# Rotary embedding on one core: the first loads put in one queue behind a 1 MB piece of x, and a small store put ahead of the scalar queue

## The chip, the core and the metric

The kernel runs on one NeuronCore of one Trainium2 chip. The metric is the device time of one execution in microseconds (us): the median of 5 runs. Besides these there is one profiled execution, with a trace of every instruction and of every packet that the core's 16 DMA engines moved. Clock times in this text are microseconds from the start of the profiled span.

## What is computed

The input x has the shape (8, 2048, 8, 64): batch, position, head, element, in float32. The tables cos and sin have the shape (2048, 32). Each head vector of 64 is cut into two halves of 32 and rotated; out has the shape of x.

```python
x1 = x[..., : x.shape[-1] // 2]
x2 = x[..., x.shape[-1] // 2 :]
out1 = x1 * cos - x2 * sin
out2 = x1 * sin + x2 * cos
return np.concatenate([out1, out2], axis=-1)
```

That is 33.55 MB of x read, 33.55 MB of out written, and 0.5 MB of tables read. Every output element needs two products and one sum.

## The kernel before

**Tiles.** The 2048 positions of a batch are spread over 128 partitions, 16 consecutive positions each, so a partition's share of a batch is one contiguous row of 32 KB. A *slab* is half of this for one batch: 8 positions, 4096 floats per partition, 2 MB in all. There are 16 slabs, numbered 0 to 15 in the order of work: first the lower half of all 8 batches, then the upper half (L58). A slab lives in one of 9 buffers `xt` (NBUF, L34), is rotated in place, and is stored from the same buffer. So load 9 has to wait until store 0 has left its buffer, load 10 for store 1, and so on.

**Units.** A slab is rotated in two *units* of 2048 floats per partition (UNIT = 4·HD, HD = 512). Only the first slab (in pieces of HD, HD, 2·HD and UNIT) and the last slab (UNIT, 2·HD, HD, HD) are cut finer (`pieces`, L67). Slab 0 is also loaded in four pieces, 256 KB, 256 KB, 512 KB and 1 MB (`cuts`, L62); every other slab is one load of 2 MB.

**Who does what.** For an ordinary unit (kind A) GpSimd (POOL) makes the two cross products x2·(−sin) and x1·sin into `t2` (L138, two instructions, one with `sin_sb`, one with `nsin`), VectorE (DVE) makes the product of x and cos into `t1` (L144; `cos_ps` is a copy of cos in PSUM, made at L108), and DVE adds the two back into `xt` (L151). In slabs 5 and 10 the sums are made otherwise (L114 to 116): for the first unit (kind C) DVE makes both products (L144, L161), for the second (kind B) DVE makes one and POOL the others; in both, TensorE adds them by products with an identity matrix into PSUM (L156, L157, L172, L173), and ScalarE (ACT) copies the sums back into `xt` (L158, L176). The table `nsin` = −sin is made by ACT (L106).

**Queues.** Loads of x and of sin are issued by SyncE (SP) on its queue, which the profile calls q1 (L84, L89). The load of cos (L92) and all stores (L183) are issued by ACT on its queue, q10. Both queues run on the same 16 DMA engines. A 2 MB transfer is 128 packets of 16 KB, 8 on each engine; a 256 KB transfer is 128 packets of 2 KB.

**Order.** Each engine works through its instructions in order. ACT therefore issues no store while it stands at the copies of slab 5 or of slab 10; the stores behind them, of slabs 3 and 8 and later, are issued right after the last copy. DVE's order is fixed by `keep`, L143 to L164: product, sum, product, sum, unit after unit. The order on POOL is the planner's. The completion of a DMA is counted on one of eight semaphores, which are dealt out in turn, and a DMA waits until the former DMA on its semaphore has landed.

Of the kernel before, what the change touches and what calls it, by code (L numbers as in the profile page):

```python
# [10 lines left out]
def kernel(  # L11
# [7 lines left out]
    nc = tc.nc  # L19
    keep = tc.keep_in_program_order  # L20
    f32 = mybir.dt.float32
    PSUM = bass.MemoryType.PSUM

    B, S, H, D = x.shape
    Dh = D // 2
    P = 128
    HD = H * D
    R = S // P
# [3 lines left out]
    SLAB = SL * HD  # L32
    UNIT = 4 * HD
# [4 lines left out]
    ov = out.rearrange("b (q r) h d -> b q (r h d)", q=P)  # L38
    cos_src = cos.rearrange("(q r) d -> q r d", q=P)
    sin_src = sin.rearrange("(q r) d -> q r d", q=P)  # L40

    const_pool = ctx.enter_context(tc.tile_pool(name="const", bufs=1))
# [7 lines left out]
    cos_sb = const_pool.tile([P, R, Dh], f32, tag="cb")  # L50
# [8 lines left out]
    last = len(slabs) - 1  # L59
    xts = {}  # L60

    def cuts(i):  # L62
        if i == 0:
            return [HD, HD, 2 * HD, UNIT]
        return [SLAB]

    def pieces(i):  # L67
        if i == 0:
            return [HD, HD, 2 * HD, UNIT]
        if i == last:  # L70
            return [UNIT, 2 * HD, HD, HD]
        return [UNIT, UNIT]

    def spans(sizes):
        lo = 0
        for n in sizes:
            yield lo, n
            lo += n

    def load(i):  # L80
        b, l = slabs[i]
        xt = xpool.tile([P, SLAB], f32, tag="xt", name=f"xt{i}")
        for lo, n in spans(cuts(i)):
            nc.sync.dma_start(  # L84
                out=xt[:, lo : lo + n],
                in_=xv[b, :, l * SLAB + lo : l * SLAB + lo + n],
            )
            if i == 0 and lo == 0:
                nc.sync.dma_start(out=sin_sb, in_=sin_src)  # L89
        xts[i] = xt  # L90

    nc.scalar.dma_start(out=cos_sb, in_=cos_src)  # L92
    for i in range(NBUF):
        load(i)

# [2 lines left out]
        out=eye,  # L98
        in_=eye,
# [80 lines left out]
    def store(i, lo, n):  # L180
        b, l = slabs[i]
        keep(
            nc.scalar.dma_start(  # L183
                out=ov[b, :, l * SLAB + lo : l * SLAB + lo + n],
                in_=xts[i][:, lo : lo + n],
            )
        )

    for i in range(last + 1):
        if i == last:  # L190
            for k in range(i - LAG, i):
                store(k, 0, SLAB)
        for lo, n in spans(pieces(i)):
            rotate(i, lo, n)
            if i == last:
                store(i, lo, n)
        if LAG <= i < last:
            store(i - LAG, 0, SLAB)
        if i > LAG and i - LAG - 1 + NBUF <= last:
            load(i - LAG - 1 + NBUF)  # L200
# [30 lines left out]
```

## Time and profile before

| | |
|---|---|
| median of 5 runs | 164.75 us (164.72 to 164.92) |
| the profiled execution's own time | 164.73 us |
| its span in the trace | 162.9 us |
| busy share of the span | DVE 88%, POOL 86%, PE 19%, ACT 7% |
| moved by DMA | 67.66 MB, mean 415 GB/s over the span |
| first instruction of DVE (copy of cos) | 4.89 us |
| first product of POOL | 5.56 us |
| last instruction of DVE ends | 154.79 us |

The profile is read from the outside inwards. The span says how long the traced part lasts; 1.8 us of the run's time lie around it. Then come the busy shares by engine, and the share of the DMA engines in 40 equal slices of the span. A table by stretch gives, for each stretch of time, the busy time of each engine, the granted clock of TensorE, and at its end the mean busy share of the 16 DMA engines and what they moved in GB/s. The DMA view cut to a stretch tells how many packets each queue moved in it. The timeline lists instructions with start and duration; a bracket behind an instruction is the idle time of its engine just before it, and what ended it.

### The profile page before, as it was taken

To read this page: it belongs to the slowest core of one execution; us is meant where nothing else is said; L and a number is where in the kernel's file an instruction comes from. 1 tells how busy PE (TensorE), PEld (TensorE's weight loads), DVE (VectorE), ACT (ScalarE), POOL (GpSimd) and SP (SyncE) were. 2 spreads that over 40 slices of the span, in tenths; PEclk is the share of its full clock that TensorE was granted. 3 is DMA by queue.
4 is the path that set the end of the run, shared out by engine and by line. 5 is a ranking of instruction groups with operands and counts; after the bars stand their busy time and mean duration, and the time that the engine had idled before them with its cause. 6 is when DMAs were issued, how large, how long until landed. Compare 5 with 4: busy or idle time off the path is not lost. (4 is left out here: it accounts for less than half of the span.)

```text
span 162.9 us, 480 instructions
## 1 busy us (share of the span) xinstructions
PE 31.7 (19%) x64; PEld 12.9 (8%) x64; DVE 143.4 (88%) x71; ACT 12.0 (7%) x20; POOL 139.3 (86%) x74
## 2 busy tenths in 40 slices
PE   0000000000000079991000000899900000000000
PEld 0000000000000024440000000344300000000000
DVE  0687999999999999999899999999999999999900
ACT  3300000000000002431000000033210000000000
POOL 1699999999999999799999999956999999995000
PEclk9999999999999999999655555599995555555555
DMA  5999999999999999999999999999999999999995
GB/s 157 372 432 438 414 398 426 418 450 426 418 442 430 426 430 446 422 418 446 422 416 450 424 418 442 442 426 418 446 426 414 446 430 426 430 446 426 414 413 212
DMA packets 5763, 67.66 MB, mean 415 GB/s; under 512 B 640, under 2 KB 640, under 8 KB 1664
## 3 DMA queue, kind: packets, MB, share of 16 engines
q1 hardware_dynamic: 2880, 33.82, 49.6%
q10 hardware_dynamic: 2880, 33.82, 48.7%
q14 instruction: 3, 0.02, 0.0%
HBM read 34.08 MB, written 33.55 MB: 415 GB/s over the span
## 5 line engine op out<-in xcount | busy, mean ns | idle before, releaser
L138 POOL TENSOR_TENSOR t<-xt,sin_sb 128x1024 f32<-128x1024 f32 (+2 forms) x34 | 70.9, 2085 | 10.7 <-DVE xt L151 6.3
L144 DVE TENSOR_TENSOR t<-xt,cos_ps 128x2048 f32<-128x2048 f32 (+2 forms) x36 | 73.9, 2056 | 1.0
L138 POOL TENSOR_TENSOR t<-xt,nsin 128x1024 f32<-128x1024 f32 (+2 forms) x34 | 70.9, 2085 | 0.0
L151 DVE TENSOR_TENSOR xt<-t,t 128x2048 f32<-128x2048 f32 (+2 forms) x32 | 64.8, 2025 | 5.5 <-POOL t L138 2.0
L172 PE MATMUL o<-t,eye 128*128 128x512 f32 x16 | 10.2, 726 | 86.4 <-DVE t L144 86.4
L176 ACT COPY xt<-o 128x512 f32<-128x512 f32 x8 | 4.7, 586 | 93.7 <-PE o L173 93.7
L172 PEld LDWEIGHTS o<-t,eye 128*128 128x128 f32 x16 | 3.6, 238 | 90.7 <-issue 90.7
L156 PE MATMUL o<-t,eye 128*128 128x512 f32 x16 | 8.2, 592 | 0.0
L157 PE MATMUL o<-t,eye 128*128 128x512 f32 x16 | 8.2, 592 | 0.0
L173 PE MATMUL o<-t,neye 128*128 128x512 f32 x8 | 5.7, 799 | 0.2 <-DVE t L161 0.2
L158 ACT COPY xt<-o 128x512 f32<-128x512 f32 x8 | 4.7, 586 | 9.0 <-PE o L157 9.0
L108 DVE COPY cos_ps<-cos_sb 128x512 f32<-128x512 f32 x1 | 0.7, 695 | 4.9 <-DMA cos_sb<-in_cos_dram 4.9
L161 DVE TENSOR_TENSOR t<-xt,sin_ps 128x2048 f32<-128x2048 f32 x2 | 4.6, 2280 | 0.0
L173 PE MATMUL o<-t,eye 128*128 128x512 f32 x8 | 4.1, 592 | 0.0
L156 PEld LDWEIGHTS o<-t,eye 128*128 128x128 f32 x16 | 3.0, 190 | 3.8 <-issue 3.8
L157 PEld LDWEIGHTS o<-t,eye 128*128 128x128 f32 x16 | 3.0, 190 | 3.8 <-issue 3.8
L173 PEld LDWEIGHTS o<-t,neye 128*128 128x128 f32 x8 | 1.8, 252 | 4.3 <-issue 2.7
L173 PEld LDWEIGHTS o<-t,eye 128*128 128x128 f32 x8 | 1.5, 190 | 1.9 <-issue 1.9
L106 ACT ACT_TABLE_LOAD x1 | 1.3, 1283 | 1.2 <-PEq L215 1.2
L106 ACT ACTIVATE nsin<-sin_sb 128x512 f32<-128x512 f32 x1 | 0.6, 630 | 3.0 <-DMA sin_sb<-in_sin_dram 3.0
L109 ACT COPY sin_ps<-sin_sb 128x512 f32<-128x512 f32 x1 | 0.6, 579 | 0.0
L96 POOL MEMSET eye<- 128x128 f32 x1 | 0.2, 205 | 0.3 <-POOLq L215 0.3
(6 smaller groups left out, 1.0 us busy)
## 6 DMA issues: line engine op xcount, KB each, us to landing
xt<-in_x_dram SPq DMA_DIRECT2D x15, 2048.0 KB, 29.5
out_dram<-xt ACTq DMA_DIRECT2D x15, 2048.0 KB, 16.1
xt<-in_x_dram SPq DMA_DIRECT2D x1, 1024.0 KB, 7.6
out_dram<-xt ACTq DMA_DIRECT2D x1, 1024.0 KB, 10.5
xt<-in_x_dram SPq DMA_DIRECT2D x2, 256.0 KB, 4.2
xt<-in_x_dram SPq DMA_DIRECT2D x1, 512.0 KB, 5.6
out_dram<-xt ACTq DMA_DIRECT2D x1, 512.0 KB, 9.1
out_dram<-xt ACTq DMA_DIRECT2D x2, 256.0 KB, 7.7
```

What stands on the lines that cost most here:

```text
L106: nc.scalar.mul(nsin, sin_sb, -1.0)
L108: nc.vector.tensor_copy(cos_ps, cos_sb)
L138: nc.gpsimd.tensor_mul(out=t2u[:, :, u, :].rearrange("p (r h) d -> p r h d", h=H), in0=xu[:, :, 1 - u, :].rearrange("p (r h) d -> p r h d" ...
L144: nc.vector.tensor_mul(out=t1.rearrange("p (r k d) -> p r k d", r=nr, d=Dh), in0=xk, in1=rep(cos_ps[:, r0 : r0 + nr, :], 2 * H),)
L151: keep(nc.vector.tensor_add(out=xt, in0=t1, in1=t2))
L156: nc.tensor.matmul(o, eye, t1[:, cs], start=True, stop=False)
L157: nc.tensor.matmul(o, eye, t2[:, cs], start=False, stop=True)
L158: keep(nc.scalar.copy(xt[:, cs], o))
L161: nc.vector.tensor_mul(out=t2.rearrange("p (r k d) -> p r k d", r=nr, d=Dh), in0=xk, in1=rep(sin_ps[:, r0 : r0 + nr, :], 2 * H),)
L172: nc.tensor.matmul(o, eye, t1u[:, gs, u, :], start=True, stop=False)
L173: nc.tensor.matmul(o, eye if u else neye, t2u[:, gs, 1 - u, :], start=False, stop=True)
L176: keep(nc.scalar.copy(xu[:, gs, u, :], o.rearrange("p (g d) -> p g d", d=Dh)))
```

## The change

The load of cos moves from ACT's queue to SP's queue. On SP's queue the order becomes: the first 1 MB of slab 0, cos, sin, the second 1 MB of slab 0, then the slabs as before. Slab 0 is rotated in pieces of 2·HD, 2·HD and UNIT, the last slab in UNIT, 2·HD and 2·HD, and the last slab is stored in two transfers of 1 MB instead of 1 MB, 512 KB, 256 KB and 256 KB. A tile of zeros is set by DVE, and ACT's queue begins with a store of 16 x 16 zeros (64 bytes from each of 16 partitions) to a place in out that the store of the last slab writes later.

```diff
+    zero = const_pool.tile([P, 16], f32, tag="zero")
+    nc.vector.memset(zero, 0.0)
+    nc.scalar.dma_start(out=ov[B - 1, 0:16, R * HD - 16 : R * HD], in_=zero[0:16, :])
+
     def cuts(i):
-        if i == 0:
-            return [HD, HD, 2 * HD, UNIT]
-        return [SLAB]
+        return [UNIT, UNIT] if i == 0 else [SLAB]
 
     def pieces(i):
         if i == 0:
-            return [HD, HD, 2 * HD, UNIT]
+            return [2 * HD, 2 * HD, UNIT]
         if i == last:
-            return [UNIT, 2 * HD, HD, HD]
+            return [UNIT, 2 * HD, 2 * HD]
         return [UNIT, UNIT]
...
             if i == 0 and lo == 0:
+                nc.sync.dma_start(out=cos_sb, in_=cos_src)
                 nc.sync.dma_start(out=sin_sb, in_=sin_src)
         xts[i] = xt
 
-    nc.scalar.dma_start(out=cos_sb, in_=cos_src)
     for i in range(NBUF):
         load(i)
...
         for lo, n in spans(pieces(i)):
             rotate(i, lo, n)
-            if i == last:
-                store(i, lo, n)
+            if i == last and lo == 0:
+                store(i, 0, UNIT)
+        if i == last:
+            store(i, UNIT, UNIT)
```

In the built program of the changed kernel POOL's first products come in another order. Before, they were, piece by piece of slab 0, sin then nsin: s0, n0, s1, n1, s2, n2, s3, n3. Now they are s0, s1, n0, n1, s2, n2, with pieces of twice the size. The order on DVE is as written: product and sum of piece 0, product and sum of piece 1, and so on. From slab 1 on, the orders on all engines are those of before.

## The prediction

> **What bounds the kernel now.** I began with the page's slices of the span, because two engines stand near 90% and the DMA queues move 67.66 MB.
>
> ```profile
> DMA  5999999999999999999999999999999999999995
> GB/s 157 372 432 438 414 398 426 418 450 426 418 442 430 426 430 446 422 418 446 422 416 450 424 418 442 442 426 418 446 426 414 446 430 426 430 446 426 414 413 212
> ```
>
> The DMA engines are never idle between the second slice and the last. The chain that ended last names DVE for 17% and DMA for 13%, but it ends with DVE at 154.79, and 8 us of span follow in which only stores run. So the transfers set the end, and the second view is the table by stretch: where do they move less than their usual rate?
>
> ```profile
> 1.50:3.00 1.50, 0.00 (x0) 0.00 (x0) 0.00 (x0) 0.94 (x1) 0.00 (x0) 1.00 0.63 149
> 3.00:4.50 1.50, 0.00 (x0) 0.00 (x0) 0.00 (x0) 0.00 (x0) 0.00 (x0) 1.00 1.05 395
> 4.50:6.00 1.50, 0.00 (x0) 0.00 (x0) 1.07 (x2) 0.56 (x2) 0.44 (x1) 1.00 1.04 306
> 6.00:9.00 3.00, 0.00 (x0) 0.00 (x0) 2.17 (x4) 0.79 (x3) 3.00 (x5) 1.00 1.04 406
> 18.00:22.00 4.00, 0.00 (x0) 0.00 (x0) 3.90 (x2) 0.00 (x0) 4.00 (x2) 1.00 1.02 381
> 80.00:117.00 37.00, 14.48 (x30) 6.20 (x31) 36.19 (x17) 3.86 (x7) 33.64 (x16) 0.65 1.01 431
> 124.00:156.00 32.00, 0.00 (x0) 0.00 (x0) 29.62 (x17) 0.00 (x0) 24.72 (x15) 0.50 1.00 429
> ```
>
> The last two columns are the DMA share and GB/s. Full rate is 431. Against it the stretches lose (431 - rate)/431 of their length: 0.98, 0.13, 0.44 and 0.17 us up to 9 us, and 0.46 us at 18 to 22, when the first store joins the loads. Elsewhere almost nothing is lost, so about 2 us is all that the transfers could gain.
>
> The third view is the timeline, for the other bound. DVE and POOL run without a pause from slab 1 on, so a late start of theirs is still there at slabs 5 and 10, where ACT stands at its copies and the stores wait behind them.
>
> ```profile
> 5.56 0.73 POOL L138 TENSOR_TENSOR t<-xt,sin_sb 128x256 f32<-128x256 f32 x1 [4.25 <-DMA sin_sb<-in_sin_dram]
> 17.67 2.30 DVE L144 TENSOR_TENSOR t<-xt,cos_ps 128x2048 f32<-128x2048 f32 x1
> 73.88 0.59 ACT L158 COPY xt<-o 128x512 f32<-128x512 f32 x1 [1.13 <-PE o L157]
> 73.89 1.85 ACTq L183 DMA_DIRECT2D out_dram<-xt  x4
> 118.44 1.86 ACTq L183 DMA_DIRECT2D out_dram<-xt  x4
> ```
>
> At 73.89 and 118.44 ACT issues the stores of slabs 3 and 8. How long could they be late before the DMA engines run dry? The DMA view, cut to 118.4 to 121.3 and to 121.3 to 122.7, answers for the second:
>
> ```profile
> q1 hardware_dynamic: 80, 1.31, 105.4%
> q10 hardware_dynamic: 2, 0.00, 0.0%
> ...
> q10 hardware_dynamic: 25, 0.41, 68.2%
> q1 hardware_dynamic: 19, 0.15, 25.0%
> ```
>
> Columns: packets, MB, share. The new store moves nothing until 121.3; the last load has 0.15 MB left then, 0.35 us at full rate. All loads are done after that. So without the store the engines would have been dry at about 121.7.
>
> **The change part by part.**
>
> *Transfers, start.* Before, four transfers of 2 KB packets lead; now 8 KB packets do, with only the tables' 512 KB in 2 KB packets. The first 0.98 us of loss (first packets on their way) I keep. Of the other 0.74 us I let 0.5 go, since a queue of bigger packets is not short of work; bounds 0 (if the gap at 4.5 to 6 comes from something else) and 0.74.
>
> *Transfers, first store.* The first store is issued at 17.66; from 17.7 to 21.5 the DMA view shows q1 packets alone, 384 GB/s. No such loss shows at 73.89 (423 GB/s from 72 to 77), so it belongs to the first store to out or on that path. The store of zeros has 16 rows and may pay it at the start. There it either overlaps the 0.98 us that is lost anyway (gain 0.46) or delays the loads by as much (gain 0). I take half, 0.23.
>
> *Transfers, end.* The last 1 MB leaves in 8 KB packets rather than 4 KB and 2 KB. 395 against 431 GB/s on 0.5 MB of 2 KB packets is 0.11 us; I take 0.1. Sum of the transfers' lead: 0.5 + 0.23 + 0.1 = 0.8 us.
>
> *Issues.* SP issues cos as well, 0.40 us on ACT in the row of before, ahead of sin, the second half of slab 0 and all later loads; the first 1 MB takes 2.4 us to move, so the queue behind it is never empty and this costs nothing. ACT's zero store waits for a small memset on DVE; behind it stand only the table load and nsin, which waits for sin anyway. Load 4 waits for the zero store's semaphore; its turn comes after 20 us, so that wait is covered unless that store takes over 15 us.
>
> *Compute, start.* POOL starts when sin has landed. Before, three transfers of 256 KB had to pass; now 1.5 MB, which is 0.79 MB more, 1.82 us at 431 GB/s. POOL's start P becomes 5.56 + 1.82 = 7.4; bounds 6.9 (if the 2 KB ramp's loss goes) and 7.9 (if the zero store costs its 0.46 here). POOL's products of 128x512 followed each other by 1.22 us before (8.28, 9.50, 10.71), those of 128x1024 by 2.29. DVE's first sum needs n0, the third of the new order: it ends at P + 2.44 + 1.25 = P + 3.7. From there DVE works without a wait: sum (1.24), product and sum of piece 1 (1.27 each, n1 is ready), product of the unit (2.3) and, with the pauses of some 0.03 to 0.1 between, the sum from P + 9.95 (n2 has ended at P + 9.47) to P + 12.25. So the first product of slab 1 starts at P + 12.27 = 19.65, against 17.67: DVE is 2.0 us late (bounds 1.5 and 2.5), and stays so, since slab 1 and later are unchanged and DVE has no pauses there to make it up.
>
> *What that costs.* Nothing, while transfers are queued. The stores of slab 8 are issued at 118.44 + 2.0 = 120.44. At an empty queue a transfer takes about 0.9 us to its first packets (SP's first issue at 0.74, first bytes in the stretch 1.5 to 1.75; cos, issued at the same time, about 1.3). They are ready at 121.3 to 121.7. The loads run dry at 121.7 less the lead. So the stores can be 2.4 us late at most without loss; with 2.0 us, the lead that survives this place is 0.4 us of the 0.7 that exists there. At slab 3 the same sum (0.31 MB left at 77.1, so dry at 77.8; issue 73.89) leaves 3.0 us; it does not decide. At the end, DVE's last three pieces take 0.45 us less (two instructions fewer), it ends at 156.3, and the last 1 MB store is ready at 157.2; its turn comes at about 158.6. Covered.
>
> *Sum.* 164.73 - 0.4 - 0.1 = 164.2 us; the profiled execution is within 0.02 us of the median of runs, so that is also the forecast for it.
>
> A rule beside this: the stores of 17.66, 73.89 and 118.44 waited 3.9, 3.3 and 2.9 us for their first packets while loads were queued. [...]
>
> **Rivals.**
>
> *Full gain.* The zero store takes the whole 0.46 us, the start all of 0.74, and DVE is only 1.5 us late, because the loads start sooner. Then the transfers lead by 1.2 us, and of that 2.4 - 1.5 = 0.9 survives slab 8: 164.73 - 0.9 - 0.1 = 163.7. For it: the big packets lead. Against it: it needs all at once.
>
> *Only moved.* The losses at 4.5 to 6 and 18 to 22 stay or reappear elsewhere, the lead is 0.1 to 0.2: 164.6.
>
> *Late stores: slower.* If the 2.9 to 3.9 us from issue to first packet is a fixed delay of a store and not the queue in front of it, the stores of slab 8 come 2.0 us later whatever the loads do. At 118.44 there is then only 0.35 us of cover; the rest, 1.65 us, is dry DMA time, less 0.1 at the end and plus the lead, which is lost too: 164.73 + 1.65 - 0.1 = 166.3. It decides from 0.35 us of lateness on. For it: both late places show about 3 us. Against it: a load issued at 84.41, into an empty q1 while q10 was busy, moves next to nothing in the stretch up to 87.8 either (9 packets, 0.02 MB), while the first load of all needed 0.9; so it is the other queue's packets that delay, not a store's nature. A milder form, DVE 2.5 us late and 1.3 us to the first packet, leaves 2.0 us of cover for 2.5 of lateness: 164.73 + 0.5 - 0.1 = 165.1.
>
> **How the numbers follow.** Forecast (164.0 to 164.5) 0.42, full gain 0.15, only moved or no change (164.5 to 165.05) 0.25, late stores 0.18. What a measurement of this kernel can tell from no change is about 0.2%, 0.33 us: faster is below 164.42. The forecast's upper edge reaches past it, so faster 0.42 - 0.06 + 0.15 = 0.51; same 0.25 + 0.06 - 0.02 = 0.29; slower 0.18 + 0.02 = 0.20. The range runs from 163.5, the full gain less 0.2 for the coarse reading of the dry time at a window's edge, to 165.6, where the milder late stores are in and half of the full late case is out.
>
> **What would show it.** Right: POOL's first product near 7.4, slab 1's first product on DVE near 19.65, the stores of slabs 3 and 8 issued near 75.9 and 120.4; 4.5 to 6 and 18 to 22 above 400 GB/s; no stretch under 90% DMA share around 77 and 121. Wrong: a dry stretch there (late stores), a loss of 0.4 us that stays at the first store (the zero store does not pay it), or a DVE that makes up its lateness before slab 5.

## The result and the profile after

The changed kernel takes 165.53 us (median of 24 runs, 164.69 to 169.5) against 164.75 us before (43 runs beside them). The ratio is 1.0045 with a 95% interval of 1.0033 to 1.0057: slower by 0.45%, where I had forecast 164.2 us. The profile that was taken first of the changed kernel is of a disturbed execution (169.5 us, one DMA engine ends 3 us behind the next), so all lines here are of the run *again*, the same kernel: profiled 165.36 us, span 163.5 us. Line numbers of the changed kernel are two above those of before (L144 is L146).

In the page's slices, the DMA engines are again busy from the second slice to the last:

```profile
DMA  5999999999999999999999999999999999999996
GB/s 192 411 451 417 441 309 417 437 433 433 421 441 433 425 433 433 437 417 437 433 429 427 437 415 429 437 429 425 425 385 409 449 405 429 449 405 429 449 385 257
```

Slice two is better than before (411 against 372), slice six is much worse (309 against 398, at 20.4 to 24.5 us), and so is slice 30 (385, at 118.5 to 122.6 us). The table by stretch, with the stretches of before and three more (last two columns: DMA share, GB/s):

```profile
1.50:3.00 1.50, 0.00 (x0) 0.00 (x0) 0.00 (x0) 1.11 (x1) 0.00 (x0) 1.00 0.85 224
3.00:4.50 1.50, 0.00 (x0) 0.00 (x0) 0.00 (x0) 0.00 (x0) 0.00 (x0) 1.00 1.02 427
4.50:6.00 1.50, 0.00 (x0) 0.00 (x0) 0.00 (x0) 0.00 (x0) 0.00 (x0) 1.00 0.95 352
6.00:9.00 3.00, 0.00 (x0) 0.00 (x0) 1.92 (x2) 1.31 (x3) 1.86 (x2) 1.00 1.08 455
18.00:22.00 4.00, 0.00 (x0) 0.00 (x0) 3.86 (x3) 0.00 (x0) 4.00 (x3) 1.00 1.02 401
22.00:26.00 4.00, 0.00 (x0) 0.00 (x0) 3.97 (x2) 0.00 (x0) 4.00 (x3) 1.00 0.99 328
121.00:122.00 1.00, 0.58 (x2) 0.00 (x0) 1.00 (x1) 0.38 (x1) 1.00 (x1) 1.00 0.77 328
122.00:123.00 1.00, 0.00 (x0) 0.00 (x0) 0.97 (x2) 0.20 (x1) 1.00 (x2) 1.00 0.63 262
124.00:156.00 32.00, 0.00 (x0) 0.00 (x0) 30.86 (x16) 0.00 (x0) 26.20 (x14) 0.50 1.00 426
```

Before, the stretches 22 to 26, 121 to 122 and 122 to 123 moved 414, 377 and 508 GB/s. So the start gained, the first store to out lost more than that stretch ever had, and at 121 to 123 the engines were partly dry. The timeline has the lateness of the compute:

```profile
7.14 2.47 POOL L140 TENSOR_TENSOR t<-xt,sin_sb 128x512 f32<-128x512 f32 x2 [5.84 <-DMA sin_sb<-in_sin_dram]
10.85 1.22 DVE L153 TENSOR_TENSOR xt<-t,t 128x1024 f32<-128x1024 f32 x1 [2.66 <-POOL t L140]
19.43 2.29 DVE L146 TENSOR_TENSOR t<-xt,cos_ps 128x2048 f32<-128x2048 f32 x1
75.39 3.60 ACTq L185 DMA_DIRECT2D out_dram<-xt  x4
121.68 2.23 ACTq L185 DMA_DIRECT2D out_dram<-xt  x3
```

POOL starts 1.6 us later than before, DVE's first sum stands 2.66 us for the third product of POOL, and DVE reaches slab 1 1.76 us later. The stores of slab 3 are issued 1.5 us later and those of slab 8 3.24 us later. The DMA view of 121 to 123 us, 40 slices of 0.05 us in which a packet is counted where it starts, shows the result:

```profile
DMA  9997970077797777700000000000009997000000
```

From 121.85 to 122.5 us no engine starts a packet: the loads are done and the stores of 121.68 have not come yet. A packet of 16 KB usually took 0.61 us, and by the packets the engines stood idle for up to 1.25 us here, some 0.55 us in the mean.

### The profile page after: what moved, and what is told of

The parts are those of the page before. It is cut to its first block, busy times and chain, and to the rows that moved or that the text cites. A ratio compares the mean times of both kernels' runs of the same rounds, so it can differ in the third digit from the quotient of the medians.

```text
span 167.6 us, 462 instructions
## 1 busy us (share of the span) xinstructions
PE 33.7 (20%) x64; PEld 13.5 (8%) x64; DVE 142.8 (85%) x68; ACT 12.0 (7%) x20; POOL 138.6 (83%) x70
## 5 line engine op out<-in xcount | busy, mean ns | idle before, releaser
L140 POOL TENSOR_TENSOR t<-xt,sin_sb 128x1024 f32<-128x1024 f32 (+1 forms) x32 | 70.1, 2191 | 10.7 <-DMA sin_sb<-in_sin_dram 5.6
L146 DVE TENSOR_TENSOR t<-xt,cos_ps 128x2048 f32<-128x2048 f32 (+1 forms) x34 | 73.5, 2168 | 1.0
L140 POOL TENSOR_TENSOR t<-xt,nsin 128x1024 f32<-128x1024 f32 (+1 forms) x32 | 70.1, 2193 | 0.0
L153 DVE TENSOR_TENSOR xt<-t,t 128x2048 f32<-128x2048 f32 (+1 forms) x30 | 64.5, 2149 | 6.1 <-POOL t L140 2.6
L174 PE MATMUL o<-t,eye 128*128 128x512 f32 x16 | 11.7, 824 | 87.0 <-DVE t L146 87.0
L158 PE MATMUL o<-t,eye 128*128 128x512 f32 x16 | 8.2, 592 | 0.0
L159 PE MATMUL o<-t,eye 128*128 128x512 f32 x16 | 8.2, 592 | 0.0
L175 PE MATMUL o<-t,neye 128*128 128x512 f32 x8 | 6.2, 866 | 0.1
L175 PE MATMUL o<-t,eye 128*128 128x512 f32 x8 | 4.1, 592 | 0.0
L158 PEld LDWEIGHTS o<-t,eye 128*128 128x128 f32 x16 | 3.0, 190 | 3.8 <-issue 3.8
```

The costliest lines, as they stand in the source:

```text
L140: nc.gpsimd.tensor_mul(out=t2u[:, :, u, :].rearrange("p (r h) d -> p r h d", h=H), in0=xu[:, :, 1 - u, :].rearrange("p (r h) d -> p r h d" ...
L146: nc.vector.tensor_mul(out=t1.rearrange("p (r k d) -> p r k d", r=nr, d=Dh), in0=xk, in1=rep(cos_ps[:, r0 : r0 + nr, :], 2 * H),)
L153: keep(nc.vector.tensor_add(out=xt, in0=t1, in1=t2))
L158: nc.tensor.matmul(o, eye, t1[:, cs], start=True, stop=False)
L159: nc.tensor.matmul(o, eye, t2[:, cs], start=False, stop=True)
L174: nc.tensor.matmul(o, eye, t1u[:, gs, u, :], start=True, stop=False)
```

## The experiments

Each row below is one kernel: the start of DVE's first product of slab 1; when the stores of slabs 3 and 8 were issued; the loss of the DMA engines in three places of its profile; the profiled time; median and ratio to the kernel before on the same chip. A loss here is the length of a stretch less the usual time of the packets in it (16 KB 0.611, 8 KB 0.309, 4 KB 0.159, 2 KB 0.084 us), the mean of 16 engines: *start* from the first packet (1.72 to 1.76 us) to 9 us, *first store* 18 to 27 us, *late* 72 to 124 us, the last as the difference to before. For after_held, whose first packet comes at 2.98 us, the start is counted from where that of the others begins. All in us. A profile is one execution: those of after_nozero and after_11 lie below the median of their runs, that of after_order is its slowest run.

| kernel | DVE slab 1 | stores 3 / 8 | start | first store | late | profiled | median, ratio |
|---|---|---|---|---|---|---|---|
| before | 17.67 | 73.89 / 118.44 | 1.33 | 0.48 | 0 | 164.73 | 164.75 |
| again | 19.43 | 75.39 / 121.68 | 0.63 | 1.20 | 0.71 | 165.36 | 165.36, 1.0026 (1.001 to 1.0042) |
| after_nozero | 19.25 | 75.64 / 120.02 | 0.70 | 1.19 | 0.16 | 164.93 | 165.25, 1.0026 (1.0003 to 1.0049) |
| after_cosact | 19.24 | 76.00 / 120.58 | 0.62 | 0.98 | 0.53 | 165.24 | 165.35, 1.0025 (1.0002 to 1.0048) |
| after_order | 18.99 | 76.51 / 121.09 | 0.60 | 1.32 | 0.67 | 166.35 | 165.28, 1.0031 (1.0013 to 1.0048) |
| after_11 | 19.35 | 75.44 / 120.03 | 0.67 | 1.04 | 0.16 | 164.64 | 165.35, 1.0036 (1.0011 to 1.0062) |
| after_held | 20.68 | 77.45 / 121.83 | 1.80 | 1.11 | 0.59 | 166.44 | 166.33, 1.0104 (1.0074 to 1.0133) |
| after_early | 16.86 | 73.80 / 118.17 | 0.66 | 0.74 | 0 | 164.24 | 164.38, 0.9980 (0.997 to 0.9991) |
| before_zero | 17.72 | 74.00 / 118.34 | 1.18 | 0.57 | 0 | 164.80 | 165.29, 1.0013 (0.9999 to 1.0026) |
| before_tail | 17.60 | 74.09 / 118.64 | 1.35 | 0.28 | 0 | 164.63 | 164.88, 1.0003 (0.9994 to 1.0012) |
| before_cossp | 18.52 | 75.26 / 119.81 | 1.11 | 0.80 | 0 | 165.43 | 165.35, 1.0025 (1.0007 to 1.0044) |
| before_late | 18.52 | 76.20 / 120.75 | 1.23 | 0.62 | 0.49 | 165.51 | 164.98, 1.0005 (0.9992 to 1.0019) |
| before_late3 | 20.46 | 76.98 / 121.53 | 1.44 | 0.53 | 0.96 | 165.54 | 166.15, 1.0071 (1.0054 to 1.0088) |
| before_1mb | 19.02 | 75.60 / 119.97 | 0.63 | 1.07 | 0.31 | 165.05 | 165.40, 1.003 (1.001 to 1.0051) |
| before_512 | 17.98 | 74.30 / 118.64 | 0.70 | 0.85 | 0 | 164.31 | 164.62, 0.9983 (0.9974 to 0.9993) |
| again_512 | 18.27 | 74.86 / 119.20 | 0.71 | 0.74 | 0 | 164.27 | 164.47, 0.9991 (0.9975 to 1.0008) |
| before_512_11 | 18.22 | 74.68 / 119.02 | 0.83 | 0.77 | 0 | 164.39 | 164.62, 0.9994 (0.9983 to 1.0005) |
| before_10 | 18.70 | 74.85 / 119.20 | 0.92 | 0.73 | 0 | 164.59 | 164.59, 0.9998 (0.9982 to 1.0014) |
| before_12 | 18.05 | 74.89 / 119.44 | 1.30 | 0.53 | 0 | 164.70 | 164.82, 1.0006 (0.9995 to 1.0016) |

My theory after the result was that the stores of slabs 3 and 8 come too late for the DMA queues. The rival was that one of the transfers at the start (the zero store, cos on the sync queue, the large first piece) makes the loss by itself.

**again**, the changed kernel unchanged.

> The changed kernel once more, unchanged, for a profile whose time is near the median of 165.5. Late stores: POOL's first product near 6.9, slab 1's first product on DVE near 19.2, the stores of slabs 3 and 8 issued near 76.3 and 120.9, and a DMA share under 0.9 for some 0.5 to 1 us near 77 to 79 or 121 to 124. Zero store to blame: no such dip, but a loss at the start or at the first store that before doesn't have. Time 165.5 in both.

Measured 165.36 us. Slower once more, and the spread of the changed kernel is wider (164.8 us upwards) than that of before.

**after_nozero**, the change without the store of zeros:

```diff
-    zero = const_pool.tile([P, 16], f32, tag="zero")
-    nc.vector.memset(zero, 0.0)
-    nc.scalar.dma_start(out=ov[B - 1, 0:16, R * HD - 16 : R * HD], in_=zero[0:16, :])
```

> The changed kernel without its store of zeros. Late stores: 165.3 to 165.6, as the changed kernel, since DVE is as late as there. Zero store to blame: 164.3 to 164.8, the loss goes. If the store of zeros had helped at the first store: 165.7 to 166.

165.25 us, a first store of 1.19 us. Without the zero store the first real store loses as much as with it.

**before_zero**, the kernel before with the same three lines behind the load of cos.

> The kernel before, with the store of zeros added behind cos on the scalar queue. Late stores: 164.75 as before, or 164.3 if the zeros pay for the loss at the first store (381 GB/s at 18 to 22). Zero store to blame: 165.2 to 165.6.

First store 0.57 against 0.48 us, median 165.29 us with a ratio whose interval takes in 1. Neither way does the zero store pay for the first store, which is what my term of 0.23 us stood on. The median by itself lies where I expected it if the zero store were to blame (165.2 to 165.6 us); what speaks against that is after_nozero, which is as slow without the store. Why this median lies above the profiled 164.80 us I can't say.

**before_late**, the kernel before with one product of POOL ahead of the others, into a tile that nobody reads, and **before_late3** with three, of which this is the edit:

```diff
+    late = const_pool.tile([P, R, Dh], f32, tag="late")
+    for _ in range(3):
+        keep(nc.gpsimd.tensor_mul(out=late, in0=sin_sb, in1=sin_sb))
```

> The kernel before, with one more product of 128x512 on POOL ahead of its first one (1.25 us, into a tile that nobody reads); its result is not used. The loads are those of before, only the compute is later, by some 1.3 us. Late stores: 165.2 to 166. If lateness is hidden behind queued transfers, as I forecast (2.4 us of cover): 164.75.

> The kernel before with three more products of 128x512 on POOL, whose result is not used, ahead of and among its first ones; DVE some 3.3 us late. Late stores with 2.4 us of cover at 118.44: stores of slab 8 issued near 122, a dry stretch of 1 to 1.5 us there, time 165.7 to 166.3. If lateness never costs: 164.75 to 165.

With DVE 0.85 us late the median is 164.98 us, no difference that can be told (its profile, 165.51 us, is of one of the slower runs); with DVE 2.79 us late it is 166.15 us, 0.71% slower. Here every transfer is that of before, so lateness by itself makes the kernel slower. Its first store, issued 2.8 us later, still loses only 0.53 us: the first store's loss is not made by lateness. Where the lateness shows, in the table by stretch and the timeline of before_late3:

```profile
86.00:90.00 4.00, 0.00 (x0) 0.00 (x0) 3.86 (x3) 0.00 (x0) 4.00 (x2) 0.50 1.03 389
76.98 7.39 ACTq L186 DMA_DIRECT2D out_dram<-xt  x5
```

and the same stretch before:

```profile
86.00:90.00 4.00, 0.00 (x0) 0.00 (x0) 3.90 (x2) 0.00 (x0) 4.00 (x3) 0.50 1.00 428
```

428 against 389 GB/s: most of the loss isn't where the late stores are issued but 10 us further on, where load 12 starts up beside them. There some 16 packets of the store queue took up to 0.6 us longer than the usual 0.611, which is 0.5 us in the mean of the engines. Another 0.26 us is lost at 77.8 to 80 us, where the late stores of slab 3 have their first packets: seven of these are longer too, by up to 0.9 us.

**after_cosact**, the change with cos on the scalar queue, behind the zero store (not ahead of it, as the expectation says), and **before_cossp**, the kernel before with cos on the sync queue behind the first 256 KB:

```diff
+    nc.scalar.dma_start(out=cos_sb, in_=cos_src)
...
             if i == 0 and lo == 0:
-                nc.sync.dma_start(out=cos_sb, in_=cos_src)
                 nc.sync.dma_start(out=sin_sb, in_=sin_src)
```

> The changed kernel with the load of cos back on the scalar queue, ahead of the zeros; x and sin as changed. Cold queue (the first transfer of 128 packets on the scalar queue costs its loss at whatever time it comes, and 16 small packets don't pay it): the loss at 18 to 26 us falls from 1.2 to about 0.6 us, time 164.6 to 164.9. Late stores alone: DVE is as late as in the changed kernel, so 165.3 to 165.5.

> The kernel before with the load of cos moved to the sync queue behind the first 256 KB of x, nothing else. Cold queue: the loss at 18 to 26 us grows from 0.6 to about 1.2 us and the time to 165.3. Late stores alone: sin lands 0.1 us later at most, 164.75 to 165.

165.35 us both. Where cos is loaded doesn't decide it: the changed kernel stays slow with cos back on its queue. That before_cossp is slow as well isn't explained by its losses (none late). The losses are means of the 16 engines, but the time ends with the last engine, and the engines end unevenly. In before_cossp the last packet ends at 162.46 us and the engines in the mean at 161.2; in before these are 161.78 and 161.0, in after_order 163.10 and 161.7, in again 162.07 and 162.0. So the last engine is 0.1 to 1.4 us behind the mean, and most of the 0.6 and 0.8 us by which the profiled times of before_cossp and after_order lie above what their losses give is this. Why the engines end so far apart I leave open.

**after_order**, the change with POOL's order kept as written (sin, nsin, sin, nsin):

```diff
-                nc.gpsimd.tensor_mul(
+                keep(nc.gpsimd.tensor_mul(
```

> The changed kernel with POOL's first products in the order sin, nsin, sin, nsin of pieces 0 and 1. DVE's first sum no longer waits for the second sin product: DVE about 0.5 us late rather than 1.6. Late stores: the dry stretch near 122 is gone in every run, time 164.9 to 165.2. Cold queue alone: 165.2 to 165.4, the first store's loss stays at 1.2 us.

DVE reaches slab 1 0.44 us sooner than in again, the time stays: 165.28 us. No dry stretch shows near 122 us in its profile, and still the time isn't the 164.9 to 165.2 us that I expected with that.

**after_held**, the change with the first load held back by a memset of DVE on the same buffer (128x1024, work that the change doesn't have) and the loads kept in the order as written:

```diff
+        if i == 0:
+            nc.vector.memset(xt[:, 0:HOLD], 0.0)
```

> The changed kernel with its first load held back by a memset of 128x1024 on DVE into the same buffer, so that all loads start about 1 us later. In the ten profiles so far the loss of the transfers up to 9 us and that at 18 to 27 us (the first store) add up to 1.9 to 2.4 us, whichever is large. Time limit (the loads are held to a fixed amount by about 27 us, so what is gained at the start is lost at the first store): the loss at 18 to 27 us falls from 1.2 to 0.3 or 0.5 us and the time stays at 165.4 to 165.7. Two separate losses: 1.2 us stays, time 166.2 to 166.6.

The first load is issued 1.25 us later than in again, and all that follows with it. The start loses 1.80 us instead of 0.63, the first store still 1.11 us, and the time is 166.33 us, 1.0 us more. So the first store's loss isn't a limit on how far loads may get by a certain time, or a later start would have made it smaller. Counted from its own first packet, the start of after_held loses 0.65 us, as again's does.

**before_1mb** is the kernel before with slab 0 loaded in two pieces and POOL's order kept, **before_512** with three, **before_tail** with the end of the change alone (last slab in UNIT, 2·HD, 2·HD and two stores). The first lines of the two loads:

```diff
-            return [HD, HD, 2 * HD, UNIT]
+            return [UNIT, UNIT]            # before_1mb
+            return [2 * HD, 2 * HD, UNIT]  # before_512
```

> The kernel before with slab 0 loaded in two transfers of 1 MB, cos on the scalar queue and all pieces as before, POOL's order of before kept. Loss goes over: start 0.8 us instead of 1.7, first store 1.1 instead of 0.5, and DVE about 1.2 us late; time 164.9 to 165.3. If the first store's loss belongs to cos on the sync queue or to the coarser pieces: it stays at 0.5 and the time is 164.2 to 164.5.

> The kernel before with slab 0 loaded as 512 KB, 512 KB, 1 MB, sin behind the first; a step half way. DVE about 0.5 us late, so stores of slabs 3 and 8 below the lateness from which loss was seen. Loss goes over: 164.6 to 165. If a start gain can be kept when the stores are in time: 164.2 to 164.5, faster than both kernels.

> The kernel before with the end of the changed one alone: last slab rotated as UNIT, 2 HD, 2 HD and stored in two transfers of 1 MB. By my sum 0.1 us faster, 164.6 to 164.8. If one 1 MB store at the end lets the slowest DMA engine finish later: 164.9 to 165.2.

The large first piece alone makes the kernel as slow as the whole change does: 165.40 us, start 0.63, first store 1.07, DVE 1.35 us late. The 512 KB piece keeps nearly all of the start's gain with DVE 0.31 us late: 164.62 us, ratio 0.9983. The table by stretch of before_512 has both sides of it, the start (332 before) and the first store (408 before):

```profile
1.50:9.00 7.50, 0.00 (x0) 0.00 (x0) 2.94 (x5) 2.29 (x4) 3.12 (x5) 1.00 1.01 382
18.00:27.00 9.00, 0.00 (x0) 0.00 (x0) 8.76 (x4) 0.00 (x0) 9.00 (x5) 1.00 0.99 380
```

The end of the change is worth nothing that can be told: 164.88 us beside 164.88, where the interval of the ratio (0.9994 to 1.0012) would hide 0.1 us.

Two things were open then: why the first store's loss goes with how slab 0 is loaded (0.3 to 0.6 us where 256 KB lead, 0.85 where 512 KB, 1.0 to 1.3 where 1 MB), and whether lateness is the whole of the slowdown. Four kernels vary the number of DMAs on the sync queue and the leading piece apart:

```diff
+ after_11:       [UNIT, 2 * HD, 2 * HD]
+ before_12:      [HD, HD, 2 * HD, 2 * HD, 2 * HD]
+ before_512_11:  [2 * HD, HD, HD, UNIT]
+ before_10:      [HD, 3 * HD, UNIT]
```

> The changed kernel with the second 1 MB of slab 0 loaded as 512 KB and 512 KB, so that the sync queue takes one DMA more before the first store. If the number of DMAs in the sync queue decides the first store's loss (18 to 27 us), the loss falls from 1.2 us to about 0.5 to 0.9 us and the time to about 164.8 to 165.1 us. If the size of the leading piece decides, the loss stays at 1.0 to 1.2 us and the time at 165.3 to 165.5 us.

> The kernel before with the last 1 MB of slab 0 loaded as 512 KB and 512 KB: one DMA more in the sync queue, the leading piece of 256 KB kept. If the number decides, the first store's loss moves away from 0.5 us (cos on the sync queue also made one DMA more, and gave 0.8 us): about 0.8 us and 165.1 us. If the size of the leading piece decides, the loss stays at 0.3 to 0.6 us and the time at 164.8 us.

> The kernel before with slab 0 loaded as 512 KB, 256 KB, 256 KB and 1 MB: a leading piece of 512 KB with the number of DMAs of before. If the number decides, the first store's loss is 0.5 us and not the 0.85 us of the three-piece load led by 512 KB; the start keeps most of its gain, and the time is 164.1 to 164.4 us, the best so far. If the leading piece decides, the loss is 0.85 us and the time 164.6 us.

> The kernel before with slab 0 loaded as 256 KB, 768 KB and 1 MB: the leading piece of 256 KB kept, one DMA fewer. If the number decides, the first store's loss rises to 0.85 to 1.2 us and the time to 165.1 to 165.5 us. If the leading piece decides, the loss stays at 0.3 to 0.6 us and the time at 164.7 to 164.9 us.

First stores of 1.04, 0.53, 0.77 and 0.73 us. The number of DMAs falls: one more left the changed kernel at 1.04 and the kernel before at 0.53. The size of the leading piece fits three of the four, but before_10, led by 256 KB, lies between (0.73). What the loss does follow, roughly, is the gain of the start: 0.3 to 0.6 us where the start loses 1.2 to 1.4 (before_cossp: 0.8 at 1.1), 0.7 to 0.85 where it loses 0.7 to 0.9, 1.0 to 1.3 where it loses 0.6 to 0.7. Both together are 1.81 us before and 1.83 in again, and 1.4 to 2.0 in all other kernels but after_held (2.91), whose first packet was made later by force.

**after_early**, the change without lateness. The two products of POOL for the first piece of slab 0 are left out, and DVE's sum of that piece adds x itself; all transfers are those of the change. In the first piece out is then not the rotated x:

```diff
+        lone = i == 0 and lo == 0
-        if kind != "C":
+        if kind != "C" and not lone:
...
-            keep(nc.vector.tensor_add(out=xt, in0=t1, in1=t2))
+            keep(nc.vector.tensor_add(out=xt, in0=t1, in1=xt if lone else t2))
```

> The changed kernel with less work at its start: the two products of POOL for the first piece of slab 0 are left out, and DVE's sum of that piece adds x itself in their place, so that POOL is done with slab 0 about 2.5 us sooner; all transfers are those of the changed kernel. DVE's first product of slab 1 should start near 17.0 us (19.4 us in the changed kernel, 17.67 before). If lateness makes the changed kernel slower, the losses behind 72 us go, the first store's loss of 1.1 to 1.3 us stays and only cancels the gain at the start, and the time is 164.5 to 164.9 us, the time before. If something else makes it slower, the time stays at 165.2 to 165.5 us. If my first forecast had only missed the lateness, the lead of the start would survive and the time would be 164.2 us or less.

164.38 us, ratio 0.998, and the runs lie between 164.21 and 164.8 us. Its timeline and its table by stretch:

```profile
16.86 2.29 DVE L147 TENSOR_TENSOR t<-xt,cos_ps 128x2048 f32<-128x2048 f32 x1
73.80 1.89 ACTq L186 DMA_DIRECT2D out_dram<-xt  x4
118.17 1.92 ACTq L186 DMA_DIRECT2D out_dram<-xt  x4
```

```profile
18.00:27.00 9.00, 0.00 (x0) 0.00 (x0) 8.72 (x5) 0.00 (x0) 9.00 (x5) 1.00 0.99 388
117.00:126.00 9.00, 1.07 (x3) 0.19 (x1) 8.74 (x5) 0.58 (x1) 9.00 (x5) 0.68 1.01 433
```

and the last stretch in again:

```profile
117.00:126.00 9.00, 4.58 (x11) 1.71 (x9) 8.74 (x5) 1.81 (x4) 8.93 (x5) 0.90 0.94 397
```

117 to 126 us moves 433 GB/s (397 in again), and all late loss is gone. The same transfers are 1.0 us faster by the medians, 0.8 us by the two ratios to before, once DVE reaches slab 1 2.57 us sooner, which is 0.81 us ahead of before. That it has to be ahead isn't the point: before_512, before_512_11, before_10 and before_12 have DVE 0.3 to 1.0 us late and lose nothing behind 72 us either. The first store still loses 0.74 us, so that is a loss of its own, but smaller than the 1.2 us of again. My expectation of 164.5 to 164.9 us was too high by that.

**again_512**, before_512 once more.

> The three-piece load of slab 0 led by 512 KB in the kernel before, once more: it gave 164.62 us and a ratio of 0.9983, while its two relatives with a leading piece of 512 KB in four pieces and of 256 KB in three gave 0.9994 and 0.9998. If the gain is real, the ratio is again 0.998 to 0.999 with an interval below 1; if it was chance, the interval takes in 1.

164.47 us, ratio 0.9991 with an interval from 0.9975 to 1.0008. Two profiles of 164.27 and 164.31 us against 164.73 speak for a small gain, but only one of two intervals lies below 1. A version that beats both kernels by 0.1 to 0.2% is likely, not shown.

## Why the prediction was wrong, step by step

- **Transfers set the end**: right. after_early and before_512 gain (ratios 0.998 and 0.9983) where the transfers gain.
- **Start, 0.5 us (0 to 0.74)**: right in its place, 0.70 us measured. Part of it came from 1.5 to 3 us (149 to 224 GB/s), which I had kept as lost; 4.5 to 6 us reached 352 GB/s, not 400.
- **First store, "I take half, 0.23"**: wrong in sign. The loss grew from 0.48 to 1.20 us. The store of zeros changes nothing there (after_nozero 1.19), so no run shows the mechanism that I priced; the bounds of 0 to 0.46 left out a loss, with no reason for it. The loss goes roughly with the start's gain and is as large in again.
- **End, 0.1 us**: not shown; before_tail gives no difference, but could not tell 0.1 us.
- **POOL's start 7.4, DVE's first product of slab 1 at 19.65**: 7.14 and 19.43, inside the bounds. DVE is 1.76 us late where I said 2.0; the chain of durations held.
- **"The stores of slab 8 are issued at 118.44 + 2.0 = 120.44"**: failed. They were issued at 120.02 to 121.68 us in the profiles of again and of the variants of the change whose DVE is 1.6 to 1.8 us late. The lateness of DVE isn't passed on one to one, because the copies of ACT wait for TensorE (9.0 us in all ahead of those of L158 on the page of before), whose clock comes up at different times. The table by stretch of again and of before, 106 to 111 us (third column from the right: granted clock):

```profile
106.00:111.00 5.00, 4.94 (x7) 2.04 (x7) 4.91 (x4) 0.58 (x1) 3.80 (x2) 0.54 1.00 423
```

```profile
106.00:111.00 5.00, 5.00 (x13) 2.21 (x12) 4.91 (x3) 1.76 (x3) 2.07 (x1) 1.00 0.98 419
```

  Clock 0.54 against 1.00: 7 matmuls against 13, one copy against three. Cut to half-microsecond stretches, the table has the full clock 3.2 us (after_11), 3.4 (before), 4.0 (before_late3), 5.3 (after_early) and 6.4 us (again) behind the first matmul of slab 10, with 3.2 us between the ends. The lengths themselves come in steps: in all 20 traces the full clock lasts 13.65 or 17.07 us at a time and the half clock between the two bursts 27.31 or 30.72 us, which is 4, 5, 8 and 9 times 3.41 us. What sets the wait for the full clock isn't shown.

  Which wait a run met shows in its mean granted clock, without a trace. In the five profiled runs with a mean under 0.79 the full clock at slab 10 came 5.3 to 6.4 us behind the first matmul, in the other fifteen 3.2 to 5.0 us. The changed kernel, four variants of it and before_1mb, all with DVE 1.3 to 1.8 us late, have 91 runs under 168 us: the 38 with a mean under 0.79 have a median of 165.51 us, the other 53 one of 165.06. This speaks for the wait for the full clock as a part of the slowdown, not the whole; in the runs of before the same difference goes either way, by up to 0.3 us.
- **Slab 8, cover 2.4 us**: about right. Stores issued at 121.09 (after_order) and 121.53 us (before_late3) lost 0.06 and 0.12 us between 117 and 124, at 121.68 (again) 0.59. Cover ends some 3 us behind 118.44.
- **Slab 3, "leaves 3.0 us; it does not decide"**: wrong. No kernel whose stores of slab 3 were issued up to 75.26 us lost anything behind 72 us; from 75.4 on all of them lose there: 0.1 to 0.3 us up to 75.64 (again without its dry stretch at slab 8), 0.5 to 0.7 at 76.0 to 76.5, 0.96 at 76.98 (after_held left aside, whose loads are late as well). The cover is some 1.4 us, and what ends it isn't a dry stretch at 77.8, the only thing that I had priced, but longer packets of the stores, where load 12 starts and behind it (in before_late3 from 77.8 us on as well).
- **The lead that survives, 0.4 us**: 0 in the changed kernel, since the first store takes back 0.72 of the 0.70 us. In after_early 0.67 us at the start less 0.26 at the first store, 0.41 us, survive, and its 164.24 us profiled lie 0.49 under before.
- **Rivals**: *late stores* had the right sign, and its milder form (165.1) came near, but by luck. Its 0.5 us of dry time is there in again, but it came from stores 3.24 us late behind a DVE 1.76 us late, with 0.8 us to their first packets, where the rival had 2.5, 2.5 and 1.3 us. A store's delay isn't fixed at 3 us: that of 121.68 had packets at 122.5 us, as I had taken it. *Only moved* describes the start and the first store.
- **The stores' waits of 3.9, 3.3 and 2.9 us**: by the packets of before, 4.06, 3.42 and 3.02 us from the issue to the first of them. In again the first store waited 4.45 us.

So two steps failed. The first-store term was priced as a gain of 0.23 us and was a loss of 0.72 us in again; that is 0.95 us off, and it took the start's lead away. The cost of lateness was priced at 0.4 us of that lead and nothing more. DVE's 1.76 us were right, but 0.71 us were lost between 72 and 124 us: 0.12 us between the start of load 12 and 117 us, where I had ruled out a loss, and 0.59 us at slab 8, whose stores came 1.24 us later than my sum had them. Both hang on when the compute starts: in after_early, with the same transfers, the first loss is 0.46 us smaller and the second is gone, and with them the whole slowdown (165.36 to 164.38 us). The account isn't closed to the last tenth: in again another 0.3 us is lost behind 124 us, the engines end 0.98 us later in the mean than before, and the time is 0.63 us longer, since in before the last engine is 0.8 us behind the mean and in again 0.1.

Not settled: why loads that started sooner lose more at the first store. In every kernel the loss lies in packets of loads that take longer, at most by 0.50 us (before) to 1.13 us (after_held), from 1 to 2 us behind the store's issue until about its first packets. It isn't the zero store, cos's queue, the number of DMAs, or the store's lateness alone; and in after_early it is smaller with the same loads. One thing goes with it that no run separates from the start's gain. In every kernel SP issues a load at 19.1 to 21.2 us. Where the first store is issued within 0.35 us of it, as in again (19.43 and 19.25 us), the store loses 1.0 to 1.3 us (before_late3: 0.53); where the load comes 1.3 us or more behind the store, as in before (2.3 us) and after_early (2.4 us), it loses 0.3 to 0.85 us. Nor is it settled why the store packets at 86 to 90 us get longer.

## What to carry to other kernels

Here a larger first transfer filled the DMA queues sooner (411 against 372 GB/s in slice two) and let the compute start later (POOL at 7.14 against 5.56 us). Price the two together: the one was worth some 0.4 us (after_early against before) and the other cost 0.8 to 1.0 us (again against after_early). Cover for a late store was not only the time until the queues were dry: in before_late3 most was lost 10 us further on, where load 12 started beside the stores (389 against 428 GB/s at 86 to 90 us). Look for such a place, and ask how much of the lateness in one profile comes from when the full clock came (3.2 us behind the first matmul of slab 10 in after_11, 6.4 us in again). To find out whether lateness costs, take work out at the start and leave every transfer as it is.

## What the runs showed of the hardware

- The full TensorE clock came 3.2 to 6.4 us behind the first matmul after a pause of 28 to 30 us (20 traces), so that a DVE 1.6 to 1.8 us late moved the stores of slab 8 by anything from 1.6 to 3.2 us.
- Behind the issue of the first store to out, the loads' 16 KB packets took up to 1.11 us (before), 1.42 us (again) and 1.75 us (after_held) instead of 0.611, over some 3 to 6 us. The store queue's start at 73.89 us showed nothing like it (423 GB/s).
- Where the loads gained in their start, more was lost at the first store, a part of the gain or all of it: 0.72 against 0.70 us in again, 0.37 against 0.63 in before_512, 0.26 against 0.67 in after_early. That the one causes the other isn't shown.
- One store of 1 KB at the head of the scalar queue cost and gained nothing that could be told: 165.36 us with it (again) and 165.25 without (after_nozero), with first stores of 1.20 and 1.19 us.
